# Layer 0's feed-forward of x by seven products, with the context's tokens as a stage of their own

## The chip, the cores and the metric

One Trainium2 chip, one core of it. The metric is device time of one launch, in microseconds (us); lower is better. The kernel before takes 2818.6 us, the median of three runs (2816.46 to 2821.4). The core has a matrix engine (TensorE, here PE), a vector engine (VectorE, DVE), an activation engine (ScalarE, ACT), GpSimd (POOL) and a queue engine (SyncE, SP) that issues the transfers in order. Sums are gathered in PSUM banks; a bank here holds 128 x 512 float32.

## The reference, cut to what matters

Two layers over 1024 tokens x and 256 context tokens h of width 1024, all in float32. Layer 0 mixes x and h and gives both new values; layer 1 gives only x. Each layer has six modulation vectors for x and for h, products of a condition with the columns of a 1024 x 6144 matrix.

```python
for layer in range(DEPTH):            # DEPTH = 2
    last = layer == DEPTH - 1
    mx = split(cond @ ada_w[layer] + ada_b[layer], 6)      # for x; mh the same of cond_ctx
    xn = modulate(rms(x, norm_mix[layer]), mx[0], mx[1])
    hn = modulate(rms(h, norm_mix[layer]), mh[0], mh[1])
    yx, yh = mixer(xn, hn, ..., not last)
    x = x + mx[2] * yx
    x = x + mx[5] * swiglu(modulate(rms(x, norm_ffn[layer]), mx[3], mx[4]), ffn_in[layer], ffn_out[layer])
    if not last:
        h = h + mh[2] * yh
        h = h + mh[5] * swiglu(modulate(rms(h, norm_ffn[layer]), mh[3], mh[4]), ffn_in[layer], ffn_out[layer])
return rms(x, norm_final)

def swiglu(x, w_in, w_out):           # w_in 1024 x 5632, w_out 2816 x 1024
    a, b = split(x @ w_in, 2)
    return (silu(a) * b) @ w_out
```

## The kernel before

Activations are stored with features on the 128 partitions: x[c] is [128, 8, n], eight blocks of 128 features by n tokens, for three chunks c: the halves 0 and 1 of x (n = 512) and the context 2 (n = 256). A float32 product is made of three matmuls (`mm3`, L111 to L114): each operand is cut into a high part and a remainder, and high x high, remainder x high and high x remainder are added in one PSUM bank. A weight block of 128 x 1024 (512 KB) is loaded by SP (`load_w`), its high part made by ACT (`split`, L103) and the remainder by POOL (L109) or DVE (L107). `mm_blk` runs the eight feature blocks of one weight block over one chunk, 24 matmuls.

Layer 0's end, in the order of the code:

- `MixerOut.sweep` makes the mixer's output, one block of 128 output features at a time; the first sweep is over chunk 0, the second over chunks 1 and 2 together, so the eight weight blocks are loaded twice. Each block is added to x and its squares are collected for the norm (`Rms`). `norm` puts the normalising and cutting of a chunk (line L239 and following, tiles `a`) on a list of deferred work, which later blocks pop.
- `ffn` runs over 22 blocks of 128 hidden features, and in each over the three chunks. `f_in` makes two times 24 matmuls of the first product, then SiLU (ACT, L843), the gate (DVE, L844) and the cut into `hh` and `hl`. `f_out` makes 24 matmuls of the second product, eight outputs of three, each added at once to x by DVE (L861). The three weight blocks of a hidden block are shared by the three chunks.
- `ada_bg(1)`, called after each step of `ffn`, works off one modulation block of layer 1: SP loads two halves of 256 KB, DVE makes a dot product of each with the condition (L149).
- `final0` interleaves the last hidden block with the first four weight blocks (10 to 13) of layer 1's mixer input.

Layer 1's feed-forward, for x only, already goes by seven products: each of the two matrix products is split in 2 x 2 (halves of the inner dimension by halves of x), and seven products of sums of the parts take the place of eight. The parts of the normalised x are called B11, B21, T2, T3, T1, T4, B22. `front_1` and `front_2` make the two products that can begin before the second half of x is there, the `Block` methods the other five, and a hidden block of x takes 7 x 12 = 84 matmuls in place of 96. The out stage (`fout`, 42 steps of seven products by six groups of hidden blocks, written (product, group)) makes 924 matmuls where the plain form has 1056. In it each step's operands are loaded from two buffers in DRAM, `sd` (sums of weights) and `hd` (sums of hidden values), and cut by ACT (L1675) and DVE (L1676).

A scheduler sets the order of the instructions on every engine except between `manual_schedule` marks, where the written order holds; each queue then runs in order.

Of the kernel before, what the change touches and what calls it, by code (L numbers as in the profile page):

```python
# [19 lines left out]
P = 128  # L20
D = 1024
# [18 lines left out]
def dit(ctx, tc, A, out):  # L40
# [790 lines left out]
    def ffn(l, xn, cs, after, done, final, bg=None):  # L831
        steps = [(j, c) for j in range(NJ - 1) for c in cs]
        wts, hid = {}, {}

        def f_in(j, c):
            n = CH[c][1]
            if j not in wts:
                wts[j] = [load_w(A["w_fi"][l, j, i]) for i in range(2)] + [load_w(A["w_fo"][l, j])]
            first = j == 0 and c == cs[0]
            pa = mm_blk(wts[j][0], c, xn, first)  # L840
            pb = mm_blk(wts[j][1], c, xn, False)
            s = t2k()
            ac.activation(s[:, :n], pa, AF.Silu)  # L843
            ve.tensor_tensor(s[:, :n], s[:, :n], pb, op=ALU.mult)  # L844
            hh = T(pw, [P, 512], "hh", F32R, 3)
            hl = T(pw, [P, 512], "hl", F32R, 3)
            split(hh[:, :n], hl[:, :n], s[:, :n])
            hid[j, c] = hh, hl
            run_deferred()

        def f_out(j, c, part=None):
            n = CH[c][1]
            s = slice(0, n) if part is None else part
            hh, hl = hid[j, c]
            wh, wl = wts[j][2]
            for m in range(KB):
                ps = T(pp, [P, 512], "ps")
                ms = slice(m * P, m * P + P)
                mm3(ps[:, s], wh[:, ms], wl[:, ms], hh[:, s], hl[:, s], True, True)
                xm = x[c][:, m, s]  # L860
                ve.scalar_tensor_tensor(xm, ps[:, s], mod(l, which(c), GATE_F, m), xm, op0=ALU.mult, op1=ALU.add)  # L861
                if j == NJ - 1:
                    after(c, m, s)
            if j == NJ - 1:
                done(c, s)

        for i, st in enumerate(steps):
            f_in(*st)
            if i:
                f_out(*steps[i - 1])  # L870
            if bg is not None:
                bg()
        final(f_in, f_out, lambda: f_out(*steps[-1]))

# [4 lines left out]
    for c in (1, 2):  # L879
        acts[c] = load_act(c, ocd)  # L880
        load_x_res(c)
    mo.sweep([0], acts)
# [6 lines left out]
    for typ in (GATE_M, SCALE_F, SHIFT_F, GATE_F):  # L889
        ada_queue(1, typ, ["x"])  # L890
    rm1 = {}
    xd = [T(dram, [P, 8, 512], f"xd{c}") for c in range(2)]

    def after0(c, m, s):
        if m == 0:
            rm1[c] = Rms(CH[c][1], 1024, KB, 3 if c == 1 else 0)
        rm1[c].add(x[c][:, m])
        if m == KB - 1 and c < 2:
            sy.dma_start(xd[c], x[c])

    xn1 = {}

    def done0(c, s):
        norm_apply(xn1, rm1[c], x[c], c, 1, SCALE_M, SHIFT_M)
# [46 lines left out]
    def final0(f_in, f_out, prev):  # L951
        wis = [10, 11, 12, 13]
        wt = {}

        def blk(i, c):
            wi = wis[i]
            if i not in wt:
                wt[i] = load_w(A["w_cd"][wi])
            epis[wi](0, c, mm_blk(wt[i], c, xn1, False))

        f_in(NJ - 1, 2)
        prev()
        f_in(NJ - 1, 0)
        f_out(NJ - 1, 2)
        f_out(NJ - 1, 0)
        run_deferred()
        f_in(NJ - 1, 1)
        blk(0, 2)
        f_out(NJ - 1, 1)
        blk(1, 2)  # L970
        blk(2, 2)
        blk(0, 0)
        run_deferred()
        for i, c in ((1, 0), (2, 0), (3, 2), (3, 0), (0, 1), (1, 1), (2, 1), (3, 1)):
# [202 lines left out]
    class Halves:  # L1177


        def __init__(self, *tags):  # L1180
            self.h = [T(pX, [P, 4, 512], t, F32, 2 if t == "w1" else 1) for t in tags]

        def __getitem__(self, ix):
            p, m, *s = ix
            a = m.start if isinstance(m, slice) else m
            h = a // 4
            m = slice(m.start - 4 * h, m.stop - 4 * h) if isinstance(m, slice) else m - 4 * h
            return self.h[h][(p, m, *s)]

    x = [Halves("w1", "rx"), Halves("w1", "wo")]  # L1190
# [217 lines left out]
    xr = [T(dram, [P, 8, 512], f"xr{c}") for c in range(2)]  # L1408

    def cut(hi, lo, src, leng, bias=None):  # L1410

        b = 0.0 if bias is None else bias
        ac.activation(hi, src, AF.Identity, bias=b)  # L1413
        if bias is None:
            (ve if leng == "dve" else po).tensor_tensor(lo, src, f32(hi), op=ALU.subtract)  # L1415
        else:
            ve.scalar_tensor_tensor(lo, src, b, f32(hi), op0=ALU.add, op1=ALU.subtract)

    class Seven:

        def __init__(self, l, xs_, alloc):
            self.l, self.x, self.t, self.alloc = l, xs_, {}, alloc
            sh = mods[l, SHIFT_F]
            self.sh = [sh[:, k, 0:1] for k in range(KB)]
            d = T(cst, [P, 4, 1], f"dsh{l}")
            ve.tensor_tensor(d, sh[:, 4:8, 0:1], sh[:, 0:4, 0:1], op=ALU.subtract)
            self.d = [d[:, k] for k in range(4)]

        def scaled(self, c, r, k):
            y = self.x[c][:, k]
            ve.scalar_tensor_tensor(y, y, mod(self.l, "x", SCALE_F, k), r.r, op0=ALU.mult, op1=ALU.mult)

        def new(self, name):
            self.t[name] = self.alloc(name)

        def parts(self, name, at, raws, bias=None):

            self.new(name)  # L1440
            hi, lo = self.t[name]
            todo = None
            for k in range(4):
                if at:
                    at(name, k)
                s = raws(k)
                b = bias(k) if bias else 0.0
                ac.activation(hi[:, k], s, AF.Identity, bias=b)
                if todo:
                    todo()  # L1450

                def todo(k=k, s=s, b=b):
                    if bias:
                        ve.scalar_tensor_tensor(lo[:, k], s, b, f32(hi[:, k]), op0=ALU.add, op1=ALU.subtract)
                    else:
                        ve.tensor_tensor(lo[:, k], s, f32(hi[:, k]), op=ALU.subtract)

            todo()

        def first(self, r):  # L1460
            for k in range(KB):
                self.scaled(0, r, k)
            self.parts("B11", None, lambda k: self.x[0][:, k], lambda k: self.sh[k])
            self.parts("B21", None, lambda k: self.x[0][:, k + 4], lambda k: self.sh[k + 4])

        def second(self, r, tmp, at):
            x0, x1, sh = self.x[0], self.x[1], self.sh
            t2 = {}

            def sub(o, a, b, c_):  # L1470
                ve.scalar_tensor_tensor(o, a, b, c_, op0=ALU.add, op1=ALU.subtract)
                return o

            def r2(k):
                self.scaled(1, r, k)
                self.scaled(1, r, k + 4)
                ve.tensor_tensor(x0[:, k], x1[:, k], x0[:, k], op=ALU.subtract)
                t2[k] = tmp()
# [14 lines left out]
    for m in range(KB):  # L1493
        spill(0, m)
# [502 lines left out]
```

## Time and profile before

| | |
|---|---|
| time of the runs shown, median | 2818.6 us |
| the profiled execution's own time | 2822.97 us |
| its span | 2821.2 us |
| PE busy | 2663.8 us, 94% |
| DVE busy | 1802.2 us, 64% |
| ACT busy | 1033.1 us, 37% |
| POOL busy | 668.3 us, 24% |
| DMA | 300.45 MB, 106 GB/s in the mean |

Times are counted from the span's start. The mixer's output of layer 0 lies at about 590 to 680 us, layer 0's feed-forward at 683 to 1620, layer 1's mixer at 1620 to 2150 and its feed-forward from there to the end. PE, DVE, ACT and POOL are busy with data; SP only issues. The granted clock tells how much of a stretch PE ran at the higher of its two levels (1.2 and 2.4 GHz). What an engine waited for is put down to the last thing that came.

### The profile page before, as it was taken

How to read it: one execution, taken by the hardware profiler on the slowest of the kernel's cores; microseconds unless marked ns; L12 is line 12 of the kernel's file. 1: busy time of each engine (PE TensorE's matmuls, PEld its weight loads, DVE VectorE, ACT ScalarE, POOL GpSimd, SP SyncE). 2: the span in 40 equal slices, each digit the busy share in tenths (PEclk: the TensorE clock that was granted, in tenths of full speed). 3: DMA queues.
4: the chain of work that ended last, by engine and by line, in shares of the span. 5: the costliest groups of instructions: out<-in, count | busy, mean ns of one | idle time of the engine just before them, and what ended most of it. 6: DMA issues, size and time to landing. Idle time of an engine off the chain costs nothing.

```text
span 2821.2 us, 35301 instructions
## 1 busy us (share of the span) xinstructions
PE 2663.8 (94%) x13524; PEld 2237.7 (79%) x13524; DVE 1802.2 (64%) x3170; ACT 1033.1 (37%) x1677; POOL 668.3 (24%) x438
## 2 busy tenths in 40 slices
PE   6988899999999999999999899898899899999998
PEld 4877788787888888888888788787667688888886
DVE  7769776556665555555444635887767766665555
ACT  5425455543111111111111532676654333332443
POOL 2132122352121211112111415643320121102110
PEclk8999999999999999999999899999999999999999
DMA  6343110352122122222111122113351444446653
GB/s 239 104 130 122 38 31 27 113 174 75 60 82 75 54 90 68 75 68 76 37 38 45 62 103 88 57 61 124 111 176 64 142 160 172 157 171 242 223 190 136
DMA packets 127929, 300.45 MB, mean 106 GB/s; under 512 B 12176, under 2 KB 28304, under 8 KB 126480
## 3 DMA queue, kind: packets, MB, share of 16 engines
q1 hardware_dynamic: 126512, 296.62, 31.5%
q8 instruction: 106, 1.74, 0.3%
q10 hardware_dynamic: 1248, 1.57, 0.2%
q14 instruction: 63, 0.52, 0.1%
HBM read 240.22 MB, written 57.93 MB: 106 GB/s over the span
## 4 chain that ended last, share of the span: by engine, by line
PE 68%; DVE 16%; DMA 6%; ACT 5%; issue 3%; POOL 2%; SPq 0%; DVEq 0%; ACTq 0%; POOLq 0%
PE ps L112 21%; PE ps L113 21%; PE ps L114 21%; DVE junk L149 3%; DMA adaw<-in_ada_dram 2%; PE ps L702 1%; DVE sm L1100 1%; DVE t2k L234 1%; DVE st L682 1%; DVE spt L107 1%; ACT P L685 1%; PE ps L192 1%; POOL wl L109 1%; DMA t2k<-oc 1%; ACT wh L103 1%
## 5 line engine op out<-in xcount | busy, mean ns | idle before, releaser
L112 PE MATMUL ps<-a,wh 128*128 128x512 f32 (+1 forms) x1784 | 656.5, 368 | 19.3 <-ACT a L239 6.9
L113 PE MATMUL ps<-a,wl 128*128 128x512 f32 (+1 forms) x1784 | 649.7, 364 | 10.2 <-DVE wl L107 9.1
L114 PE MATMUL ps<-a,wh 128*128 128x512 f32 (+1 forms) x1784 | 648.2, 364 | 2.4 <-DVE a L240 1.8
L109 POOL TENSOR_TENSOR wl<-raw,wh 128x1024 fp32r<-128x1024 f32 x109 | 269.0, 2471 | 863.2 <-ACT wh L103 856.7
L112 PEld LDWEIGHTS ps<-a,wh 128*128 128x128 f32 x1784 | 342.2, 192 | 78.1 <-ACT a L239 8.8
L113 PEld LDWEIGHTS ps<-a,wl 128*128 128x128 f32 x1784 | 342.2, 192 | 67.1 <-DVE wl L107 12.3
L114 PEld LDWEIGHTS ps<-a,wh 128*128 128x128 f32 x1784 | 342.0, 192 | 55.0 <-DVE a L240 3.1
L861 DVE SCALAR_TENSOR_TENSOR x<-ps,md,x 128x512 f32<-128x512 f32 (+1 forms) x528 | 312.2, 652 | 4.4 <-PE ps L114 4.4
L149 DVE CUSTOM_DVE_ANT_0 junk<-adaw,cond_x 128x512 bf16<-128x512 f32 x160 | 137.9, 862 | 171.6 <-DMA adaw<-in_ada_dram 169.7
L844 DVE TENSOR_TENSOR t2k<-t2k,ps 128x512 f32<-128x512 f32 (+1 forms) x66 | 39.3, 596 | 246.0 <-PE ps L114 246.0
L112 PE MATMUL ps<-hh,wh 128*128 128x512 f32 (+1 forms) x528 | 188.7, 357 | 3.0 <-ACT hh L103 2.1
L114 PE MATMUL ps<-hl,wh 128*128 128x512 f32 (+1 forms) x528 | 187.6, 356 | 1.1 <-DVE hl L107 1.1
L113 PE MATMUL ps<-hh,wl 128*128 128x512 f32 (+1 forms) x528 | 188.3, 357 | 0.0
L843 ACT ACTIVATE t2k<-ps 128x512 f32<-128x512 f32 (+1 forms) x66 | 34.8, 527 | 380.8 <-PE ps L114 380.8
L103 ACT ACTIVATE wh<-raw 128x1024 fp32r<-128x1024 f32 x127 | 133.9, 1056 | 108.2 <-PE ps L114 37.9
L1537 POOL TENSOR_TENSOR wo<-wo 128x512 f32<-128x512 f32 x44 | 76.9, 1749 | 403.4 <-DMA wo<-in_w_fo_dram 400.8
L112 PE MATMUL ps<-a,w 128*128 128x512 f32 x400 | 158.0, 395 | 7.6 <-ACT w L1413 6.3
L113 PE MATMUL ps<-a,w 128*128 128x512 f32 x400 | 157.8, 395 | 1.5 <-DVE w L1415 1.5
L114 PE MATMUL ps<-a,w 128*128 128x512 f32 x400 | 157.6, 394 | 0.0
L103 ACT ACTIVATE hh<-t2k 128x512 fp32r<-128x512 f32 (+1 forms) x66 | 36.8, 557 | 285.4 <-DVE t2k L844 285.4
L112 PEld LDWEIGHTS ps<-hh,wh 128*128 128x128 f32 x528 | 100.6, 190 | 18.5 <-ACT hh L103 2.6
L114 PEld LDWEIGHTS ps<-hl,wh 128*128 128x128 f32 x528 | 100.5, 190 | 15.6 <-DVE hl L107 1.5
(379 smaller groups left out, 5612.5 us busy)
## 6 DMA issues: line engine op xcount, KB each, us to landing
adaw<-in_ada_dram SPq DMA_DIRECT2D x160, 256.0 KB, 2.7
raw<-in_w_fi_dram SPq DMA_DIRECT2D x72, 512.0 KB, 3.6
hd<-t2k SPq DMA_DIRECT2D x66, 256.0 KB, 6.0
raw<-hd SPq DMA_DIRECT2D x28, 512.0 KB, 4.9
raw<-in_w_cd_dram SPq DMA_DIRECT2D x26, 512.0 KB, 3.5
raw<-in_w_fo_dram SPq DMA_DIRECT2D x22, 512.0 KB, 3.6
wo<-in_w_fo_dram SPq DMA_DIRECT2D x22, 512.0 KB, 5.4
sd<-wo SPq DMA_DIRECT2D x11, 1024.0 KB, 7.1
```

Of the source, the lines that this page charges most:

```text
L103: ac.activation(hi, src, AF.Identity)
L107: ve.tensor_tensor(lo, src, f32(hi), op=ALU.subtract)
L109: po.tensor_tensor(lo, src, f32(hi), op=ALU.subtract)
L112: te.matmul(ps, wh, xh, start=first, stop=False, skip_group_check=more)
L113: te.matmul(ps, wl, xh, start=False, stop=False, skip_group_check=more)
L114: te.matmul(ps, wh, xl, start=False, stop=last, skip_group_check=more)
L149: ve.tensor_tensor_reduce(jk[:, :512], w, cond[which][:, h * 512 : h * 512 + 512], op0=ALU.mult, op1=ALU.add, scale=1.0, scalar=0.0, accum ...
L192: te.matmul(self.ps, ones, sq[:, :n], start=self.count == 1, stop=self.count == self.total)
L843: ac.activation(s[:, :n], pa, AF.Silu)
L844: ve.tensor_tensor(s[:, :n], s[:, :n], pb, op=ALU.mult)
L861: ve.scalar_tensor_tensor(xm, ps[:, s], mod(l, which(c), GATE_F, m), xm, op0=ALU.mult, op1=ALU.add)
L1537: e.tensor_tensor(self.rows(o, o + 1), self.rows(a, a + 1), self.rows(b, b + 1), op=op)
```

## The change

Layer 0's feed-forward of x goes by seven products as layer 1's does. The classes of layer 1 (`Halves`, `Seven`, `Back`, `Block`) are moved up, take the layer as an argument, and serve both layers. Around them:

- The mixer's output takes three sweeps: chunk 0, then the context, then chunk 1; the eight weight blocks are loaded a third time. Both halves of x are stored to DRAM (`spill`, to xr00 and xr01).
- The context's tokens have a stage of their own before x's: 22 steps of two input products and one output product of 256 columns (`ctx_in`, `ctx_out`), with weight blocks loaded and cut for them alone (`ctx_load`, remainders on DVE). Its eight outputs are gathered in four PSUM banks over all 22 steps. Beside it, parts of x are prepared (`t1_raw`, `t3_raw`, T2, `pre_w`), and the modulation blocks still queued are worked off.
- Then x's front products, its parts T3, T1, T4, B22, the main stage over 22 hidden blocks (`main`), and the out stage (`out`). In the out stage the context's values are read back from DRAM and normalised, and 32 modulation blocks of layer 1 are worked off (`ada_one`: one load of 512 KB, one dot product of 1024, two buffers), two per step from step (2,4) on.
- Weight blocks 10 and 11 of layer 1's mixer input follow, then 12, 13 and the rest.

Layer 0's feed-forward weights are thus read from DRAM twice. The core of the diff:

```diff
-    for c in (1, 2):
+    for c in (2, 1):
         acts[c] = load_act(c, ocd)
         load_x_res(c)
+    sv = Seven(0, x, pX, None, 3)
...
     mo.sweep([0], acts)
     mo.w.update((m, load_w(mo.wsrc(m), "dve")) for m in range(2))
-    mo.norm(0)
-    mo.sweep([1, 2], acts)
-    mo.norm(1)
+    for m in range(KB):
+        sv.spill(0, m)
...
+    deferred.append(first0)
+    mo.sweep([2], acts)
+    mo.w.update((m, load_w(mo.wsrc(m), "dve")) for m in range(2))
+    sy.dma_start(xc0, x[2])
     mo.norm(2)
+    mo.rm[1] = Rms(512, 1024, KB, 2)
+    for m in range(KB):
+        mo.block(m, 1, acts)
+        sv.spill(1, m)
+        ada_bg(1)
...
+    def ctx_load(j, what):
+        if what == "fi":
+            t = act_tile(0, [P, 2, 2, 1024])
+            hi, lo = t[:, 0], t[:, 1]
+        else:
+            t = sv.t8([P, 2, 1024])
+            hi, lo = t[:, 0:1], t[:, 1:2]
+        for i in range(2 if what == "fi" else 1):
+            raw = T(pC, [P, 1024], "cr", F32, 3)
+            mark[0] = sy.dma_start(raw, A["w_fi"][0, j, i] if what == "fi" else A["w_fo"][0, j]).ins
+            cut(hi[:, i], lo[:, i], raw)
+        cw[what, j] = hi, lo
...
+    for j in range(NJ):
+        ctx_in(j)
+        ctx_load(j, "fo")
+        if j + 2 < NJ:
+            ctx_load(j + 2, "fi")
+        if j:
+            ctx_out(j - 1)
...
+        if 2 <= j < 6:
+            sv.t1_raw(mo.rm[1], j - 2)
+            sv.t3_raw(j - 2)
+        if j > 5:
+            ada_bg(1)
...
+    sv.second(None, None, ("T2",), True)
+    ctx_out(NJ - 1)
...
+    for j in range(3):
+        sv.front_1(j)
+        sv.front_2(j)
...
+    sv.second(None, None, ("T3",), True)
...
+    d = T(pW, [P, 8, CTX], "w34", F32, 3)
+    for m in range(KB):
+        ac.activation(d[:, m], couts[m // 2][:, m % 2 * CTX : m % 2 * CTX + CTX], AF.Identity, scale=mod(0, "c", GATE_F, m))
+    sy.dma_start(dc0, d)
...
+    sv.main(bl)
...
+    def ada_one(typ, b):
+        w = T(pX, [P, 2, 1024], "w1", F32, 2)[:, 0]
+        sy.dma_start(w.rearrange("p (h n) -> p h n", h=2), A["ada"][1, typ * KB + b].rearrange("h p n -> p h n"))
+        m_ = mod_tile(1, typ)
+        ve.tensor_tensor_reduce(adc[:, 1], w, adc[:, 0], op0=ALU.mult, op1=ALU.add, scale=1.0, scalar=0.0,
+                                accum_out=m_[:, b, 0:1])
...
+        if (i, b) > (2, 3):
+            for _ in range(2):
+                if ada_tail:
+                    ada_one(*ada_tail.pop(0))
+        if i == 6 and b in (1, 3):
+            pre_cd(10 + b // 2)
...
+    sv.out(x, [slice(0, 512)], added0, ended0, bg0)
...
-    ffn(0, xn, [0, 1, 2], after0, done0, final0, lambda: ada_bg(1))
-    ada_bg(1000)
```

What this moves on the queues, at the places where the stages meet. SP, in the changed kernel, at the end of the sweep over chunk 1 and the start of the context's stage (L827 stores a block of x, L1295 loads a weight block of the context's stage into a raw tile `cr`; a name after "waits" is what the issue waits for):

```order
L827 DMA xr01_1009_5232<-wo_967_5117 128x512 [waits DVE_49]
L1295 DMA cr_1189_6234<-in_w_fi_dram 128x1024 [waits Pool_49]
L827 DMA xr01_1009_5232<-wo_967_5117 128x512 [waits DVE_49]
L1295 DMA cr_1190_6238<-in_w_fi_dram 128x1024 [waits DMAHW4_49,PE_49]
L1295 DMA cr_1192_6243<-in_w_fi_dram 128x1024 [waits Pool_49]
```

The second half of the first weight block is issued behind the store of x's last block.

DVE in the out stage, from layer 1 in the kernel before (L1676 cuts a step's operands, L1866 adds an output to x):

```order
L1676 TENSOR_TENSOR a_3678_21742<-raw_21739,a_3678_21742 128x2048
L1676 TENSOR_TENSOR a_3680_21772<-raw_21769,a_3680_21772 128x2048
L1866 SCALAR_TENSOR_TENSOR a_3647_21437<-ps_21617,md_2148_11755,a_3647_21437 128x512
L1866 SCALAR_TENSOR_TENSOR a_3647_21437<-ps_21618,md_2148_11755,a_3647_21437 128x512
L1866 SCALAR_TENSOR_TENSOR a_3647_21437<-ps_21619,md_2148_11755,a_3647_21437 128x512
L1866 SCALAR_TENSOR_TENSOR a_3647_21437<-ps_21620,md_2148_11755,a_3647_21437 128x512
L1676 TENSOR_TENSOR tx_21806<-rx_21802,tx_21805 128x2048
```

and from layer 0 in the changed kernel (L773 is the cut, L1462 the dot product of a modulation block and its read-out):

```order
L773 TENSOR_TENSOR tx_12280<-raw_12276,tx_12279 128x2048
L1462 ISA wo_11393,md_1864_12247<-w_1865_12249,wo_11393 128x1024
L1462 ISA md_1864_12247 128x1
L773 TENSOR_TENSOR a_1872_12316<-rx_12313,a_1872_12316 128x2048
L1462 ISA wo_11393,md_1864_12247<-w_1869_12283,wo_11393 128x1024
L1462 ISA md_1864_12247 128x1
```

Between the cuts stand one or two dot products, where layer 1 has none.

SP at the same place of the changed kernel (L1053 and L1059 load a step's operands, L1460 a modulation block):

```order
L1053 DMA raw_1860_12238<-sd02_1018_5241 128x1024 [waits DMAHW4_49,DVE_49]
L1460 DMA w1_1855_12181<-in_ada_dram 128x2x512 [waits DMAHW1_49,DVE_49]
L1460 DMA w1_1858_12214<-in_ada_dram 128x2x512 [waits DMAHW2_49,DVE_49]
L1059 DMA raw_1860_12238<-hd02_1012_5235 128x1024 [waits DMAHW7_49]
L1053 DMA raw_1866_12276<-sd03_1019_5242 128x1024 [waits DMAHW0_49,Activation_49]
L1460 DMA w1_1859_12217<-in_ada_dram 128x2x512 [waits DMAHW5_49,DVE_49]
L1460 DMA w1_1863_12245<-in_ada_dram 128x2x512 [waits DMAHW6_49,DVE_49]
L1059 DMA raw_1866_12276<-hd03_1013_5236 128x1024 [waits DMAHW3_49]
```

The second load of each step's operands is issued behind two modulation loads that wait for DVE.

## Rows read from the trace of the kernel before

**Rows 1.** the profile's page, busy time of the engines, then the chain by engine

```profile
PE 2663.8 (94%) x13524; PEld 2237.7 (79%) x13524; DVE 1802.2 (64%) x3170; ACT 1033.1 (37%) x1677; POOL 668.3 (24%) x438
...
PE 68%; DVE 16%; DMA 6%; ACT 5%; issue 3%; POOL 2%; SPq 0%; DVEq 0%; ACTq 0%; POOLq 0%
```

**Rows 2.** busy time by stretch: stretch, length, engines' busy us (instructions), clock, DMA share, GB/s

```profile
core 0: us, PE busy (x) PEld busy (x) DVE busy (x) ACT busy (x) POOL busy (x), PEclk, DMA share, GB/s
550.00:690.00 140.00, 131.96 (x655) 111.39 (x655) 72.50 (x110) 59.37 (x86) 65.45 (x37) 0.98 0.47 154
690.00:823.00 133.00, 128.02 (x657) 108.13 (x656) 91.92 (x170) 29.83 (x46) 22.81 (x9) 1.00 0.19 58
823.00:1560.00 737.00, 737.00 (x3882) 637.42 (x3881) 402.65 (x696) 111.81 (x162) 132.41 (x54) 1.00 0.20 63
1560.00:1640.00 80.00, 69.54 (x308) 56.40 (x307) 50.80 (x77) 45.38 (x72) 27.13 (x21) 0.89 0.21 81
...
2150.00:2235.00 85.00, 72.19 (x289) 55.47 (x288) 68.24 (x94) 37.25 (x55) 6.52 (x5) 0.94 0.34 118
2235.00:2580.00 345.00, 345.00 (x1503) 282.30 (x1502) 222.56 (x270) 115.01 (x160) 66.89 (x39) 1.00 0.44 158
2580.00:2790.00 210.00, 209.29 (x915) 171.49 (x914) 121.55 (x85) 84.03 (x65) 22.93 (x12) 1.00 0.66 226
2600.00:2650.00 50.00, 50.00 (x222) 41.38 (x221) 23.36 (x15) 18.13 (x11) 0.00 (x0) 1.00 0.77 274
```

**Rows 3.** timeline of PE in layer 0's feed-forward: start, duration, operation; then its SiLUs

```profile
915.13 0.39 PE L114 MATMUL ps<-hl,wh 128*128 128x512 f32 x1
...
915.81 0.39 PE L114 MATMUL ps<-hl,wh 128*128 128x512 f32 x1
916.03 0.28 PE L112 MATMUL ps<-a,wh 128*128 128x256 f32 x1
...
916.27 0.28 PE L114 MATMUL ps<-a,wh 128*128 128x256 f32 x1
...
L843 ACT ACTIVATE t2k<-ps x4: 383/598/598, 905.4 to 946.7; 128x512 f32<-128x512 f32 x3, 128x256 f32<-128x256 f32 x1
```

**Rows 4.** layer 1: one line's instructions in 2340:2364, another's in 2725:2742

```profile
L1731 DVE TENSOR_TENSOR t2k<-ps,t2k x2: 690/690/691, 2343.8 to 2363.1; 128x512 f32<-128x512 f32 x2
...
L1675 ACT ACTIVATE tx<-raw x2: 1917/1918/1918, 2728.2 to 2733.6; 128x2048 fp32r<-128x2048 f32 x2
```

**Rows 5.** what PE waited for in 550:690, 1560:1640, 2150:2235: us, times, longest

```profile
PE ps L112 <- ACT a L239: 5.1, 1, 5.1
PE ps L113 <- DVE wl L107: 1.6, 1, 1.6
PE ps L112 <- ACT wh L103: 1.3, 1, 1.3
...
PE ps L112 <- ACT t2k L935: 5.6, 1, 5.6
...
PE ps L112 <- ACT w L1413: 6.3, 1, 6.3
```

**Rows 6.** cuts and dot products, by line: count, min/median/max ns, first and last start

```profile
L103 ACT ACTIVATE wh<-raw x127: 1040/1061/1078, 205.0 to 2129.0; 128x1024 fp32r<-128x1024 f32 x127
...
L109 POOL TENSOR_TENSOR wl<-raw,wh x109: 2347/2400/3801, 206.1 to 1974.4; 128x1024 fp32r<-128x1024 f32 x109
...
L107 DVE TENSOR_TENSOR wl<-raw,wh x18: 1212/1224/2299, 595.6 to 2130.1; 128x1024 fp32r<-128x1024 f32 x18
...
L1676 DVE TENSOR_TENSOR a<-raw,a x15: 2283/2292/2907, 2579.9 to 2786.1; 128x2048 fp32r<-128x2048 f32 x15
...
L340 DVE CUSTOM_DVE_ANT_0 junk<-a,cond_x x12: 1211/1220/2173, 12.5 to 52.4; 128x1024 bf16<-128x1024 f32 x12
```

**Rows 7.** DMA issues: count, KB each, median us from issue to landing

```profile
raw<-in_w_fi_dram SPq DMA_DIRECT2D x72, 512.0 KB, 3.6
...
wo<-in_w_fo_dram SPq DMA_DIRECT2D x22, 512.0 KB, 5.4
```

More of the change, by code (lines that the diff above doesn't have):

```diff
@@ L829, in norm_apply @@
         deferred.append(later)
[L831 to L873, printed above, removed]
     mo = MixerOut(0, lambda m: A["w_abo"][m])
@@ L891, in dit, with first0 @@
[L891 to L904 removed]
+    for m in range(KB):
+        sv.spill(0, m)
+    def first0():
+        mo.rm[0].finish()
+        sv.first(mo.rm[0])
@@ new lines, in dit, with at0 @@
+    sy.dma_start(dc0, d)
+    sv.load_fi(2)
+    sv.front_s(0)
+    bk.part(3)
+    sv.front_3(0)
+    bl = Block(sv, 0, bk)
+    sv.front_s(1)
+    bk.part(4)
+    sv.second(None, None, ("T1",), True)
+    bl.m6()
+    bl.m7()
+    sv.front_3(1)
+    sv.front_s(2)
+    bl.u1()
+    def at0(name, k):
+        if (name, k) == ("T4", 0):
+            bl.m5()
+        if (name, k) == ("T4", 2):
+            sv.front_3(2)
+            bl.z7()
+        if (name, k) == ("B22", 0):
+            bl.m4()
+        if (name, k) == ("B22", 1):
+            bl.c22()
@@ L906, in dit @@
+    sv.second(None, at0, ("T4", "B22"), True)
+    sv.load_fi(3)
+    sv.main(bl)
+    sM.close()
+    sW.close()
+    sB0 = es()
+    pxB = pool(sB0, "pxB")
+    x = [T(pxB, [P, 8, 512], f"xb{c}") for c in range(2)]
+    for c in range(2):
+        sy.dma_start(x[c], sv.xr[c])
+    xd = [T(dram, [P, 8, 512], f"xd{c}") for c in range(2)]
+    rm1, xn1 = {}, {}
+    rm1[0] = Rms(512, 1024, KB, 2)
+    rm1[1] = Rms(512, 1024, KB, 3)
     zd = {nm: T(dram, [P, k, 1280], f"z{nm}") for nm, k in (("rk", 2), ("rq", 2), ("rg", 4), ("rv", 4))}
@@ L1175, in dit @@
     pX = pool(sX, "pX", side="right")
[L1177 to L1190, printed above, removed]
+    x = list(halves(pX))
     t2_pool(sF, "t2j", t2k=5)
@@ L1407, in dit @@
     mo.load(1)
[L1408 to L1478, printed above, removed]
-                sub(t2[k], x1[:, k + 4], sh[k + 4], x0[:, k])
-                return t2[k]
-            self.parts("T2", at, r2)
-            self.parts("T3", at, lambda k: sub(x1[:, k], x1[:, k + 4], self.d[k], x1[:, k]))
-            self.parts("T1", at, lambda k: x0[:, k])
-            self.parts("T4", at, lambda k: sub(x0[:, k + 4], x0[:, k + 4], sh[k + 4], t2[k]))
-            self.parts("B22", at, lambda k: x1[:, k + 4], lambda k: sh[k + 4])
@@ L1882, in dit, with added1, ended1 @@
-    fout(1)
+    def added1(i, c, m, s):
+        if i in (1, 5):
+            rm1[0].add(x[0][:, m])
+        if i == 4:
+            for q_ in range(2):
+                rm1[1, q_].add(x[1][:, m, cuts[q_]])
+        if i == 6:
+            rm1[1, s.start // 256].add(x[1][:, m, s])
+    def ended1(i, s):
+        if i == 3:
+            for q_ in range(2):
+                rm1[1, q_] = Rms(256, 1024, KB, 3)
+        if i == 5:
+            done1(0, slice(0, 512), rm1[0])
+        if i == 6:
+            done1(1, s, rm1[1, s.start // 256])
@@ L1883, in dit @@
+    sv.out(x, cuts, added1, ended1)
     sA.close()
```

833 lines of the change are left out of this document (490 added, 343 removed).

## The prediction

> **What bounds the kernel now.** I read the busy line and the chain of waits first, then the busy time by stretch, the pace of TensorE (PE) inside the stretches, and last what PE waited for in the stretches that are not full. PE is busy 94% of the span, and 68% of the chain that ended last is PE [rows 1]. By stretches [rows 2]: in layer 0's feed-forward (823 to 1560 us) PE is busy for all 737 us at a granted clock of 1.00, with DMA at 0.20 and VectorE (DVE) at 403 of 737; layer 1's main stage (2235 to 2580) and its out stage (2580 to 2790) are full too. So here a matmul taken away is time taken away. The rest is at the seams. I count a stretch's loss as its length less PE's busy time, plus (1 - granted clock) x length, since at the lower of the two clock levels (1.2 against 2.4 GHz) half of the time is lost, and the share of time there is twice (1 - clock). That gives 8.0 + 2.8 = 10.8 us for 550:690, 5.0 for 690:823, 10.5 + 8.8 = 19.3 for 1560:1640, and 12.8 + 5.1 = 17.9 for 2150:2235, layer 1's change from its mixer to seven products.
>
> **Pace.** A 512-column matmul starts every 0.227 us (915.13 to 915.81 is three), a 256-column one every 0.12 (916.03 to 916.27 is two) [rows 3]. One hidden block of layer 0 has 144 of the first and 72 of the second: 32.7 + 8.6 = 41.3 us, which is the distance of the first and last SiLU of one chunk in the row of four [rows 3]. In layer 1, 84 matmuls of a hidden block take 2363.1 - 2343.8 = 19.3 us, 0.230 each, and an out step of 24 takes 2733.6 - 2728.2 = 5.4 [rows 4].
>
> **What goes.** Each hidden block of x drops from 96 to 84 matmuls of the first product: 22 x (96 x 0.227 - 19.3) = 22 x 2.44 = 53.7 us, taking layer 1's measured pace for the new code, which is the same code. The second product drops from 1056 to 924 matmuls: 132 x 0.227 = 29.9. Together -83.6 us. The 528 additions on DVE that went with every out product go too, but PE did not wait for them (DVE is at 55% there), so they count as nothing; neither do the 64 modulation blocks' halves that DVE did in that stretch.
>
> **Mixer out in three sweeps and the seam to the feed-forward.** Before, PE stood 5.1 us for the normalised x and 1.6 + 1.3 us for the first weights of the sweep [rows 5]. The norm now lies under the next sweep, so the 5.1 goes, and so does the slow start of 690:823; the 2.9 us stay. New: the context's sweep alone gives PE only 24 x 0.12 = 2.9 us per weight block, where a cut takes 1.06 on ScalarE (ACT) and 2.4 on GpSimd (POOL) [rows 6]. That fits under 2.9 with four buffers, barely: between 0 and 8 us (eight blocks of 1 us, as for a load that lands 3.6 us after its issue [rows 7] with one block of lead); I take 2. What is late next is the first weight of the context stage: in SP's order its second half stands behind the last spill of x, and its tile is free only when the sweep ends. Landing, cut and remainder are 3.6 + 1.06 + 1.22 = 5.9 us [rows 6, 7]; between 3 and 8, I take 5. So 15.8 becomes 9.9: -5.9 us.
>
> **The context's stage.** 22 steps of 72 matmuls of 256 columns, 8.6 us each, the same PE work as before, now without x's matmuls beside it. Per step three weight blocks: ACT 3 x 1.06 = 3.2, DVE 3 x 1.22 = 3.7 plus about one for the hidden values and about one for x's own preparation in some steps, and 1.57 MB in 8.6 us = 182 GB/s. The nearest row is layer 1's out stage: 226 GB/s with PE full [rows 2]. Three raw buffers and 5.9 us from issue to ready give 3 blocks per 5.9 us. Between 0 and 10 us in all; I take 1.
>
> **The change to seven products.** Layer 1's own lost 17.9 us, 6.3 of it for one cut of weights [rows 2, 5]. Here T2, the front weights and the first raw blocks are made beforehand under the context's stage; but T3, T1, T4 and B22 are made while PE waits for each, and the context's eight outputs are drained by ACT in between. Between 5 and 18; I take 12.
>
> **The out stage with 32 modulation blocks.** In the row order 27 of them lie between steps (3,0) and (5,3): 14 full steps and two halves, 14 x 5.4 + 2 x 2.7 = 81 us of PE. DVE: layer 1's out stage uses 121.6 of 210 us, so 47 of 81, and 27 dot products x 1.22 = 33 [rows 2, 6]: 80 of 81. Bytes: 226 GB/s x 81 us = 18.3 MB and 27 x 0.524 = 14.2, 32.5 MB. Where the share was 0.77 the DMAs moved 274 GB/s [rows 2], so 356 at a full share: 91 us. The two buffers: one pair takes a landing plus a dot product, 3.6 or 5.4 + 1.22 = 4.8 to 6.6 us [rows 6, 7], 13.5 pairs in 65 to 89. Three resources thus lie at the length of the stage itself, and some 11 us (two steps) are buffered ahead. A wait is added on SP: the load of the hidden sums for the step after next is queued behind two modulation loads that wait for DVE, and DVE's remainder for that step, then PE, stand behind it. Lower end 0; upper end with pair and remainder in series, (5.4 + 1.22 + 2.29) x 13.5 = 120, +39. I take 12, nearest to the DMA rows.
> The Trainium skill, "DMA: Bandwidth & Descriptors", section "Where 436 GB/s comes from", lets about 358 GB/s per core bind for HBM to SBUF, and its section on measured bandwidth has 425 for one core alone with a 16 MB transfer. The first agrees with the 356 worked out above; by 425 the 32.5 MB would need 76 us, the DMAs would not bind, and the forecast would be 2732; no row here shows such a rate.
>
> **The tail.** 19.3 us were lost at 1560:1640, 5.6 of them in one wait on ACT [rows 5]. Now the last four sums wait for squares, the first four blocks of the next projection (16.6 us on ready columns) cover the last norm, and one more weight load stands behind a store. Left: between 4 and 15; I take 9: -10.3 us.
>
> **Sum.** -83.6 - 5.9 + 1 + 12 + 12 - 10.3 = -74.8 us. The profiled execution took 2823.0 (span 2821.2 and 1.8 around it), 0.16% over the median of 2818.6; 2823.0 - 74.8 = 2748.2, in the median's terms 2744. With all terms at their lower ends: -83.6 - 9.9 + 0 + 5 + 0 - 15.3 = -104, 2715; at their upper ends: -83.6 + 3.1 + 10 + 18 + 39 - 4.3 = -18, 2801.
>
> **Rivals.**
> (a) The out stage is paced by the modulation blocks: pair and remainder in series, +39 in place of 12, 2771. For it: DVE at 80 of 81 us, two buffers, and one SP queue in which loads wait behind waiting loads. Against: the scheduler spread the pairs, and steps are cut two ahead.
> (b) Slower than before: the context's stage is paced by its weights. One mechanism: with PE giving only 8.6 us per block, three loads and their cuts go through the ring one after the other, 3 x (3.6 + 1.06) = 14 us per block [rows 6, 7]; 22 x 5.4 = +118, 2862. It decides from 8.6 + 75/22 = 12 us per block. For it: weights that x's matmuls used to cover are now read for 256 columns alone; tiles for the first product are two, freed only when a block's product ends. Against: three raw buffers, and 5.9 us from issue to ready.
> (c) The seams cost what they did: starts, transition and tail at their upper ends with the out stage at 12, -83.6 + 3.1 + 10 + 18 + 12 - 4.3 = -45, 2774. For it: each new seam brings its own starting waits and low clock (0.89 and 0.94 at the old ones [rows 2]). Against: the pieces are prepared under the stage before.
>
> **Chances.** Forecast 0.67, (a) 0.15, (b) 0.07, (c) 0.11. Its own range is 2720 to 2766; 8 in 10 with (a) and most of (c): 2720 to 2785. About 0.2% is what a measurement of this kernel can tell from no change. Faster by over that: all but (b) and a sliver between (c) and (b), 0.90; within it 0.03; slower 0.07, case (b).
>
> **What would show it.** The main stage of layer 0 with 19.3 us between its C21 additions; PE full from the second context step on, 8.6 us a step; gaps of PE in steps (3,0) to (5,3) that end with a DMA or a DVE remainder, 12 us in sum; 5 us before the first context product; about 12 us lost between the last context product and the first steady block. Wrong if context steps are over 9.2 us, if those 16 out steps take over 110 us, or if the main block's distance is over 19.8.

## The result, and the profile after

The changed kernel takes 2789.2 us in the median (2782.7 to 2794.1, four runs) against 2820.0 of the kernel before, a ratio of 0.989 with the interval 0.9865 to 0.9915. It is faster by 31 us, where 75 were forecast (2744, range 2720 to 2785). Its profiled execution took 2782.7 (span 2780.9) and is the quickest of the four; a second profile of the same kernel (below) has a span of 2790.8.

The page after: span, busy time, granted clock by slice, and the chain by engine.

```profile
span 2780.9 us, 34949 instructions
...
PE 2593.3 (93%) x13136; PEld 2167.0 (78%) x13136; DVE 1863.8 (67%) x2986; ACT 1209.7 (44%) x1859; POOL 597.8 (21%) x416
...
PEclk8999999998999999999999999999999999999999
...
PE 57%; DVE 20%; DMA 10%; issue 6%; ACT 5%; POOL 1%; SPq 1%; DVEq 0%; ACTq 0%; POOLq 0%
```

PE lost 70 us of busy time (84 went with the matmuls, but more of what is left ran at the lower clock: granted 0.974 in the mean, before 0.980), and the span only 40; DVE's share of the chain rose from 16 to 20% and DMA's from 6 to 10% [rows 1]. The stretches after, with the columns of [rows 2]:

```profile
677.00:692.00 15.00, 0.18 (x1) 0.18 (x1) 9.09 (x23) 4.23 (x5) 1.65 (x2) 0.65 0.52 178
692.00:702.00 10.00, 9.32 (x55) 9.03 (x56) 5.93 (x5) 5.77 (x6) 0.00 (x0) 0.67 0.76 256
...
820.00:893.00 73.00, 73.00 (x603) 72.37 (x601) 42.52 (x53) 36.52 (x55) 0.00 (x0) 1.00 0.53 168
...
905.00:928.00 23.00, 17.14 (x71) 13.31 (x70) 19.11 (x28) 11.65 (x18) 1.45 (x1) 0.91 0.38 137
928.00:1310.00 382.00, 380.37 (x1644) 309.31 (x1642) 241.57 (x297) 125.09 (x175) 67.56 (x40) 1.00 0.45 160
...
1327.00:1350.00 23.00, 23.00 (x103) 18.99 (x102) 9.91 (x9) 10.83 (x14) 7.54 (x7) 1.00 0.95 377
...
1475.00:1500.00 25.00, 21.07 (x88) 16.49 (x86) 20.27 (x25) 6.87 (x7) 7.46 (x3) 0.95 0.86 298
1500.00:1525.00 25.00, 20.50 (x72) 15.72 (x73) 18.60 (x15) 14.83 (x12) 4.13 (x2) 0.85 0.91 316
...
1557.00:1593.00 36.00, 29.32 (x147) 23.93 (x145) 12.23 (x18) 13.21 (x20) 4.80 (x2) 0.95 0.30 103
```

The main stage (928 to 1310) is full, and its block distance is the one that layer 1 showed [rows 4], by DVE's C21 additions (first and last start of two):

```profile
L1154 DVE TENSOR_TENSOR t2k<-ps,t2k x2: 692/692/692, 1001.0 to 1020.4; 128x512 f32<-128x512 f32 x2
```

1020.4 - 1001.0 = 19.4 us. So the 84 us of matmuls were saved as forecast; the difference is at the places that are not full. I compare each stretch with the pure time of its matmuls (0.227 and 0.12 us each; the main stage at 19.3 per block), by the starts of PE's first instruction of each stage (within the out stage by counting its matmuls), in the first and second profile of the changed kernel:

| stretch | pure work | first profile | second | lost | forecast loss |
|---|---|---|---|---|---|
| mixer output to first context product | 121.3 | 143.9 | 146.1 | 22.6, 24.8 | 9.9 |
| context's stage | 190.1 | 197.8 | 196.3 | 7.7, 6.2 | 1 |
| fronts, parts and main stage | 424.6 | 437.2 | 437.6 | 12.6, 13.0 | 12 |
| out stage, steps (3,0) to (5,3) | 81.7 | 89.8 | 93.8 | 8.1, 12.1 | 12 |
| rest of the out stage, to its last sum | 128.0 | 140.9 | 144.3 | 12.9, 16.3 | in the next line |
| first 17 blocks of the next projection | 79.7 | 91.8 | 91.9 | 12.1, 12.2 | 9 |

(121.3 is the kernel before's own 132.1 us less the 10.8 it lost there.) 76 or 85 us are lost where 44 were forecast; before it was 35. The forecast put the modulation blocks into the steps (3,0) to (5,3), and what follows them, with the waits for sums of squares, into the tail. Some 7 us of the rest of the out stage are no waiting but PE's own matmuls for these sums (L213, fifteen of about 0.46 us in the trace). What PE waited for up to the end of the context's stage, the four largest:

```profile
PE ps L113 <- ACT a L771: 15.2, 1, 15.2
PE ps L113 <- ACT wh L104: 4.7, 1, 4.7
PE ps L114 <- POOL wl L110: 3.7, 2, 2.1
PE ps L115 <- DVE ch L773: 2.5, 2, 1.5
```

and from the out stage to the next projection, the three largest (us in total, times, longest), where [rows 5] had one wait of 5.6 at the tail:

```profile
PE ps L113 <- ACT wh L104: 6.7, 1, 6.7
PE ps L213 <- POOL g L204: 4.5, 2, 3.6
PE ps L113 <- ACT a L771: 3.7, 1, 3.7
```

**The first seam.** DVE at the end of the third sweep: start, duration, line, operation.

```profile
659.12 2.77 DVE L150 CUSTOM_DVE_ANT_0 junk<-adaw,cond_c 128x512 bf16<-128x512 f32 x1
...
681.85 1.41 DVE L150 CUSTOM_DVE_ANT_0 junk<-adaw,cond_x 128x512 bf16<-128x512 f32 x1 [0.66 <-DMA adaw<-in_ada_dram]
...
683.30 0.69 DVE L150 CUSTOM_DVE_ANT_0 junk<-adaw,cond_c 128x512 bf16<-128x512 f32 x1
...
685.38 1.41 DVE L1222 SCALAR_TENSOR_TENSOR wo<-ps,md,wo 128x512 f32<-128x512 f32 x2
691.80 1.23 DVE L773 TENSOR_TENSOR a<-cr,a 128x1024 fp32r<-128x1024 f32 x1 [5.01 <-ACT a L771]
```

L1222 is the residual addition of two output blocks of the mixer. PE ended the last of them by 676.7; the additions start at 685.4, behind dot products of modulation blocks (L150), one of which waited 0.66 us for its load. Most of these take 0.69 us; the one at 659.1 and another at 663.6 took 2.77, each beside a remainder on POOL:

```profile
658.48 2.85 POOL L110 TENSOR_TENSOR wl<-raw,wh 128x1024 fp32r<-128x1024 f32 x1
```

These two are some 4 us of DVE's time ahead of the last additions; whether POOL is the cause was not tried. SP at the end of the sweep:

```profile
686.15 0.33 SPq L827 DMA_DIRECT2D xr<-wo  x1
686.53 0.42 SPq L1295 DMA_DIRECT2D cr<-in_w_fi_dram  x1
687.00 0.46 SPq L827 DMA_DIRECT2D xr<-wo  x1
```

The stores of x (L827) wait for these additions, and the first weights of the context's stage (L1295) stand between and behind them: cut on ACT at 690.7, product at 691.8. From the issue at 686.5 to the product it is 5.3 us; the rest of the wait is the late issue. After this standstill PE ran at a granted clock of 0.67 for the next 10 us, two thirds of them at the lower of its levels (1.2 GHz): an estimated 3.3 us more.

**The out stage.** DVE and then SP near the step that PE waited for:

```profile
1492.08 1.23 DVE L1462 CUSTOM_DVE_ANT_0 wo<-w,wo 128x1024 f32<-128x1024 f32 x1 [1.70 <-DMA w<-in_ada_dram]
...
1494.44 1.23 DVE L1462 CUSTOM_DVE_ANT_0 wo<-w,wo 128x1024 f32<-128x1024 f32 x1 [1.13 <-DMA w<-in_ada_dram]
...
1497.38 1.23 DVE L1462 CUSTOM_DVE_ANT_0 wo<-w,wo 128x1024 f32<-128x1024 f32 x1 [1.71 <-DMA w<-in_ada_dram]
...
1498.53 2.29 DVE L773 TENSOR_TENSOR a<-raw,a 128x2048 fp32r<-128x2048 f32 x1
```

```profile
1488.10 2.69 SPq L1460 DMA_DIRECT2D w<-in_ada_dram  x2
1490.84 0.46 SPq L1059 DMA_DIRECT2D raw<-hd  x1
1493.34 2.73 SPq L1460 DMA_DIRECT2D w<-in_ada_dram  x2
```

Each dot product (L1462) waits for its load, 1.1 to 1.7 us, and DVE's remainder of a step's operands at 1498.5 (L773) comes behind them. SP issues the next pair (1493.3) only when a dot product has given back its buffer (1493.2; the two buffers, used in turn, are called the ring below), and a step's loads stand behind or between such pairs: the one of its hidden sums was issued at 1490.8 (L1059). ACT waited for it to make the high part, and PE's two waits at this step were for both cuts:

```profile
1495.73 1.91 ACT L771 ACTIVATE a<-raw 128x2048 fp32r<-128x2048 f32 x1 [10.86 <-DMA raw<-hd]
...
PE ps L114 <- DVE a L773: 1.1, 1, 1.1
```

PE's wait of 3.7 us ended with ACT's high part (1497.6), that is with a load held up on SP's queue; 1.1 us more went to DVE's remainder behind the dot products. In the second profile the two are 6.1 and 2.3 us (the latter in two waits).

### The profile page after: what moved, and what is told of

Read it like the earlier page. It is cut to its first block, busy times and chain, and to the rows that moved or that the text cites. A ratio compares the mean times of both kernels' runs of the same rounds, so it can differ in the third digit from the quotient of the medians.

```text
span 2780.9 us, 34949 instructions
## 1 busy us (share of the span) xinstructions
PE 2593.3 (93%) x13136; PEld 2167.0 (78%) x13136; DVE 1863.8 (67%) x2986; ACT 1209.7 (44%) x1859; POOL 597.8 (21%) x416
## 4 chain that ended last, share of the span: by engine, by line
PE 57%; DVE 20%; DMA 10%; issue 6%; ACT 5%; POOL 1%; SPq 1%; DVEq 0%; ACTq 0%; POOLq 0%
PE ps L115 17%; PE ps L114 17%; PE ps L113 17%; DMA adaw<-in_ada_dram 3%; DVE junk L150 3%; DMA rx<-hd 1%; DMA w<-in_ada_dram 1%; DVE a L773 1%; PE ps L703 1%; DVE sm L1647 1%; DMA raw<-in_w_abo_dram 1%; DVE st L683 1%; DVE spt L108 1%; DMA raw<-in_w_cdo_dram 1%; ACT P L686 1%
## 5 line engine op out<-in xcount | busy, mean ns | idle before, releaser
L113 PE MATMUL ps<-a,w 128*128 128x512 f32 (+1 forms) x864 | 340.3, 394 | 14.2 <-ACT w L771 11.3
L114 PE MATMUL ps<-a,w 128*128 128x512 f32 (+1 forms) x864 | 339.5, 393 | 1.7 <-DVE w L773 1.7
L115 PE MATMUL ps<-a,w 128*128 128x512 f32 (+1 forms) x864 | 338.8, 392 | 0.0
L113 PE MATMUL ps<-a,wh 128*128 128x512 f32 (+1 forms) x680 | 265.1, 390 | 15.3 <-ACT wh L104 14.7
L114 PE MATMUL ps<-a,wl 128*128 128x512 f32 (+1 forms) x680 | 261.1, 384 | 16.3 <-DVE wl L108 10.2
L115 PE MATMUL ps<-a,wh 128*128 128x512 f32 (+1 forms) x680 | 259.1, 381 | 0.2 <-DVE a L108 0.2
L113 PEld LDWEIGHTS ps<-a,w 128*128 128x128 f32 x864 | 163.5, 189 | 51.9 <-ACT w L771 12.1
L114 PEld LDWEIGHTS ps<-a,w 128*128 128x128 f32 x864 | 163.6, 189 | 38.4 <-DVE w L773 2.8
L115 PEld LDWEIGHTS ps<-a,w 128*128 128x128 f32 x864 | 163.7, 189 | 36.2 <-DVE a L779 0.3
L773 DVE TENSOR_TENSOR w<-raw,w 128x1024 fp32r<-128x1024 f32 (+1 forms) x111 | 137.7, 1250 | 73.8 <-ACT w L771 73.8
L114 PEld LDWEIGHTS ps<-a,wl 128*128 128x128 f32 x680 | 133.5, 196 | 46.4 <-DVE wl L108 13.6
L113 PEld LDWEIGHTS ps<-a,wh 128*128 128x128 f32 x680 | 134.4, 198 | 42.6 <-ACT wh L104 16.2
L115 PEld LDWEIGHTS ps<-a,wh 128*128 128x128 f32 x680 | 133.9, 197 | 22.9 <-DVE a L108 0.6
L110 POOL TENSOR_TENSOR wl<-raw,wh 128x1024 fp32r<-128x1024 f32 x47 | 114.6, 2440 | 146.4 <-ACT wh L104 146.3
L115 PE MATMUL ps<-tx,w 128*128 128x512 f32 x352 | 140.5, 399 | 0.0
L113 PE MATMUL ps<-tx,w 128*128 128x512 f32 x352 | 138.6, 394 | 1.7 <-ACT t2k L1142 1.7
L114 PE MATMUL ps<-tx,w 128*128 128x512 f32 x352 | 138.9, 395 | 0.0
L114 PE MATMUL ps<-a 128*128 128x512 f32 (+1 forms) x324 | 128.9, 398 | 1.1 <-DVE a L773 1.1
L113 PE MATMUL ps<-a 128*128 128x512 f32 (+1 forms) x324 | 125.8, 393 | 3.7 <-ACT a L771 3.7
```

The source lines that it names most:

```text
L110: po.tensor_tensor(lo, src, f32(hi), op=ALU.subtract)
L113: te.matmul(ps, wh, xh, start=first, stop=False, skip_group_check=more)
L114: te.matmul(ps, wl, xh, start=False, stop=False, skip_group_check=more)
L115: te.matmul(ps, wh, xl, start=False, stop=last, skip_group_check=more)
L773: ve.tensor_tensor(lo, src, f32(hi), op=ALU.subtract)
```

## The experiments

All times but e11's (one run) are medians of four runs beside the kernel before on the same chip, whose medians there were 2820 to 2822; the changed kernel's is 2789. Out stage times are from its first to its last sum with the last twelve products of the main stage (+3 us), 233.7 and 241.1 us in the two profiles of the changed kernel.

**e1, no modulation blocks in the third sweep.** They go to the context's stage, where what is left of the list is worked off at the last step in place of step 10.

```diff
         sv.spill(1, m)
-        ada_bg(1)
...
+        if j == NJ - 1:
+            ada_bg(1000)
         if j == 10:
-            ada_bg(1000)
             sv.load_fi(0)
```

> The modulation blocks that stood in the mixer output's third sweep are worked off in the context's stage from its step 6 on. Theory (the dot products stand ahead of the residual additions in DVE's order, so the sweep's last additions, the stores of x and then the first weights come late): PE's wait before the first context product falls from 15.2 us to about 5, and the stretch from the start of the mixer output to that product from 143.9 us to about 133; time 9 to 12 us below the changed kernel's, about 2779. Rival (the wait is the landing and cutting of the first weights, behind the stores on SP's queue): the wait stays over 10 us and the time within 3 us of the changed kernel's.

2789.1 us, no change in the time, though the mechanism showed: the stretch to the first context product is 133.2 us in place of 143.9. PE's waits up to the end of the context's stage, two of its rows:

```profile
PE ps L115 <- DVE ch L773: 5.5, 6, 1.4
...
PE ps L113 <- ACT a L771: 3.9, 1, 3.9
```

The wait for the first weights is 3.9 us, and the context's stage now waits 5.5 for hidden values (`ch`), cut by DVE behind the same dot products: the stage takes 202.0 in place of 197.8. The out stage took 240.7, like the second profile of the changed kernel. Against that profile the edit is worth 5 us by the spans (2785.8 for 2790.8), which four runs spread over 10 do not show.

**e2, no modulation blocks in the out stage** (`ada_tail = []`).

> Left out: the 32 modulation blocks of layer 1 that the out stage works off (their results are set to zero). Theory (they are what the out stage loses): the loss of layer 0's out stage against its matmuls' pace falls from 21 us to 6 to 10 (the sums of squares at its end stay), the waits at 1494 to 1501 go; 10 to 14 us below the changed kernel, about 2777. Rival (the loss comes from the step loads themselves and from the end of the stage): at most 4 us.

2777.1 us, 12 below. The out stage took 225.9. So the 32 blocks cost 8 to 15 us there, as work that PE has to wait for. The steps (3,0) to (5,3) took 82.0 us, PE's own pace; 4.4 us of waits for sums of squares stayed at the end of the stage.

**e3, the weights behind the out stage.**

```diff
-    wpools[:] = [(pwA, 2, 1), (pwB, 2, 1)]
+    wpools[:] = [(pwB, 2, 1), (pwA, 2, 1)]
     wnext[0] = 0
     wh_ = {wi: load_w(A["w_cd"][wi]) for wi in (12, 13, 0)}
```

> The first weight block behind the out stage's four is loaded into the pool whose memory is free earlier, the other one second. Theory (PE's 6.7 us wait there is the load behind the last store on SP, into memory that the products before still used): the wait goes to under 1 us, 6 to 8 us below the changed kernel, about 2782. Rival (the wait moves to the next weight block, which is now the late one): the time stays within 2 us.

2778.9 us, 10 below. All that PE waited for from 1560 to 1660:

```profile
PE ps L213 <- POOL g L204: 0.9, 1, 0.9
```

The wait of 6.7 us for the weights is gone and no other took its place; the first 17 blocks of the next projection take 80.8 us in place of 91.8.

**e4, the modulation loads issued by GpSimd.**

```diff
-        sy.dma_start(w.rearrange("p (h n) -> p h n", h=2), A["ada"][1, typ * KB + b].rearrange("h p n -> p h n"))
+        po.dma_start(w.rearrange("p (h n) -> p h n", h=2), A["ada"][1, typ * KB + b].rearrange("h p n -> p h n"))
```

> The loads of the 32 modulation blocks in the out stage are issued by GpSimd in place of SP; the same bytes, the same dot products. Theory (PE's waits at 1494 to 1501 come from step loads queued on SP behind modulation loads that wait for their buffer): these 5 us go, about 5 us below the changed kernel, 2784. Rival (the DMAs, 0.85 to 0.95 busy there, or DVE are the limit): the time stays within 2 us, with waits in other steps.

2804.5 us, 15 above: a miss of both. SP's loads no longer stood behind the modulations, and yet the out stage took 255.6 us. DVE there:

```profile
1424.41 2.72 DVE L1094 SCALAR_TENSOR_TENSOR xb<-ps,md,xb 128x512 f32<-128x512 f32 x4
1427.05 1.22 DVE L1462 CUSTOM_DVE_ANT_0 wo<-w,wo 128x1024 f32<-128x1024 f32 x1
...
1428.30 1.23 DVE L1462 CUSTOM_DVE_ANT_0 wo<-w,wo 128x1024 f32<-128x1024 f32 x1
...
1431.99 2.29 DVE L773 TENSOR_TENSOR a<-raw,a 128x2048 fp32r<-128x2048 f32 x1 [2.45 <-ACT a L771]
...
1436.40 1.22 DVE L1462 CUSTOM_DVE_ANT_0 wo<-w,wo 128x1024 f32<-128x1024 f32 x1
```

Both dot products of a pair stand between a step's additions (L1094) and the next cut, the next follows 8 us later, and a full step of PE takes 5.4. In the stage PE waited 10.2 us for DVE's remainders of `tx`, and DVE 39.9 us for modulation blocks (15.7 and 21.2 in the two profiles of the changed kernel). But the edit changes more than SP's queue: the loads now stand in GpSimd's order among the additions of squares, for which PE waited 9.6 us (4.5 and 7.1 before the edit). So e4 does not tell what SP's order costs in the changed kernel; it shows that modulation blocks that come late hold the stage through DVE as well.

**e5, a ring of four.** The two buffers are twice as large as a block; both halves are used.

```diff
+    ring = [None]
+
     def ada_one(typ, b):
-        w = T(pX, [P, 2, 1024], "w1", F32, 2)[:, 0]
+        if b % 2 == 0:
+            ring[0] = T(pX, [P, 2, 1024], "w1", F32, 2)
+        w = ring[0][:, b % 2]
```

> In the out stage both halves of each of the two buffers hold a modulation block, so four can be under way in place of two; the same loads, bytes and dot products, on SP as before. Theory (a dot product at the head of DVE's order waits for a block that could only be asked for when a buffer came free, and the cuts of the next step stand behind it): the out stage from its first to its last product falls from 234 to 242 us to about 230, and the time is 8 to 10 us below the changed kernel, about 2780. Rival (the DMAs at 0.85 to 0.9 busy are the limit): within 3 us of the changed kernel.

2769.2 us, 20 below, twice what was expected. The out stage took 221.3. Three stretches of it, first the changed kernel's second profile, then e5:

```profile
1400.00:1450.00 50.00, 50.00 (x221) 41.17 (x220) 41.88 (x56) 18.12 (x18) 0.00 (x0) 1.00 0.82 282
1450.00:1500.00 50.00, 46.23 (x202) 37.46 (x200) 38.76 (x47) 14.76 (x11) 7.27 (x3) 1.00 0.84 299
1500.00:1550.00 50.00, 39.16 (x143) 29.67 (x144) 34.24 (x37) 27.57 (x27) 6.30 (x2) 0.83 0.60 216
```

```profile
1400.00:1450.00 50.00, 50.00 (x221) 41.17 (x220) 46.33 (x66) 21.03 (x18) 0.00 (x0) 1.00 0.95 340
1450.00:1500.00 50.00, 50.00 (x221) 41.23 (x220) 44.81 (x47) 18.97 (x15) 6.67 (x3) 1.00 0.95 345
1500.00:1550.00 50.00, 48.56 (x211) 37.57 (x210) 31.94 (x36) 25.72 (x30) 5.12 (x3) 1.00 0.39 146
```

With the same work PE is full to 1500, and the DMAs move 340 and 345 GB/s where they moved 282 and 299. They had room: the limit was how early a block could be asked for. Of the 20 us, 12 lie in the steps (3,0) to (5,3), 82.0 us for 93.8, as without the blocks (e2); 8 lie behind them. Nearly all of these steps, in the changed kernel (first profile) and in e5:

```profile
1417.00:1498.60 81.60, 77.91 (x340) 63.94 (x340) 64.59 (x80) 25.30 (x17) 7.46 (x3) 0.99 0.89 310
...
1417.00:1498.60 81.60, 81.60 (x360) 67.25 (x359) 73.12 (x86) 30.99 (x21) 6.67 (x3) 1.00 0.96 350
```

The end of the stage gains too: its waits for sums fall from 7.1 us to 1.4, and the clock stays at 1.00 from 1500 to 1550 where it was 0.83.

**e6, half of the blocks in the sweep** (`if m < 4: ada_bg(1)`, the rest in the context's stage).

> Only the first four blocks of the third sweep are followed by a modulation block; the other four are made in the context's stage, one per step from step 6 on. Theory (the dot products ahead of the last additions delay the stage, and those in the context's stage cost where DVE has no room): the stretch to the first context product is about 134 us as with none in the sweep, the context's stage takes about 2 us more than the 197.8 of the changed kernel in place of 4.2, and the time is 6 to 9 us below the changed kernel, about 2782. Rival (whatever leaves the sweep is paid back in the context's stage): within 3 us of the changed kernel.

2777.4 us, 12 below, more than expected (its runs spread from 2774.6 to 2785.7, and the profiled one is the slowest). To the first context product 134.9 us, the context's stage 199.5.

**e7, e3, e5 and e6 together.**

> The other pool for the first weight block behind the out stage, the ring of four modulation blocks and the halved sweep together. Theory: the three act at different places, so the gains add: -10 - 9 - 7 = -26, about 2763. Rival (what is gained at one seam is waited for at the next): about 2772 or more.

2752.9 us (2749.9 to 2754.7), ratio to the kernel before 0.9755 (0.974 to 0.9771): 36 below the changed kernel, more than the 26 expected and less than the 10 + 20 + 12 = 42 of the three alone. The first seam takes 132.8, the out stage 221.6, and it is the best of all versions.

```profile
span 2752.9 us, 34933 instructions
...
PE 2588.9 (94%) x13136; PEld 2165.5 (79%) x13136; DVE 1864.5 (68%) x2986; ACT 1211.2 (44%) x1859; POOL 597.8 (22%) x416
```

**e8, the changed kernel again.**

> The changed kernel once more, beside the others. Theory (its out stage runs at the edge, where a landing more or less decides, and the profiled execution was one of the quicker ones): the out stage takes 234 to 243 us, the stretch to the first context product 143 to 145, the time about 2789. Rival (the profiled execution is typical): the out stage within 1 us of 233.7.

2789.0 us; out stage 241.1, first seam 146.1. e1, e3 and e6, which leave the out stage as it is, have 240.7, 241.7 and 242.2 there: the first profile was a quick one, by 7 us.

**e9 and e10, rings of three in the sweep and the context's stage.** `adaw` gets three buffers in place of two, on e7 (e9) and on e3 with e5, the sweep left whole (e10).

> The three edits together, and in the sweep and the context's stage a ring of three modulation halves in place of two. Theory (there too a dot product that waits for its load holds up DVE's queue; PE waited 4.2 us for hidden values in the context's stage): this wait falls to about 1 us, the stage from 200 to 197 us, 2 to 4 us below the three together, about 2750. Rival (DVE's work itself is too much there, whatever the loads): no change, 2753.

2757.4 us, 4 above e7 where 2 to 4 below were expected. PE's wait for hidden values grew from e7's 4.2 us:

```profile
PE ps L115 <- DVE ch L775: 7.5, 6, 1.5
```

> The other pool for the first weight block and the ring of four in the out stage; all eight modulation blocks stay in the third sweep, but with a ring of three halves. Theory (DVE's work and its place in the queue delay the sweep's last additions, the ring only in part): the stretch to the first context product falls from 144 us to about 140, PE's wait there from 13 to 9 us; about 2756. Rival (only the two-half ring delays them): about 134 us, as with four blocks in the sweep, about 2752.

2760.0 us; 142.7 us to the first context product (expected 140, by the rival 134; e5, with rings of two there, has the same 142.7), with a wait of

```profile
PE ps L113 <- ACT a L773: 11.6, 1, 11.6
```

So at the sweep and in the context's stage a ring of three does not help. In e10 DVE waits for no load from 655 us on (3.0 us in the changed kernel), and its last additions of the sweep still start only at 684.6 (685.4): there the dot products stand in the way by their place and their work (four of at least 0.7 us per block, for x and for the context). Of the three places only the out stage was held by its ring.

**e11, the kernel before again.**

> The kernel before once more, with a profile. From the first transposes behind layer 0 to the end it took 1125.9 us in its profile, and 1130 to 1135 in ten profiles of the changed kernel and its variants. Theory (the same code, another order of loads around it: a real 4 to 6 us): 1126 again. Rival (its first profile was a quick one): about 1130.

2820.7 us; 1128.9 us from the first transposes to the end, 3.0 more than in its first profile. So a part of the distance to the 1130 to 1135 of the changed kernel and its variants is spread between executions; a real part of up to a few us is not excluded, and its cause stays open.

## Why the prediction was wrong

- The matmuls taken away: right. 84 us, with the block distance at 19.4 against 19.3. (22 x (96 x 0.227 - 19.3) is 54.8, not 53.7: a slip of 1 us.)
- The transition to seven products: 12.6 us for 12, in part by luck. By the count that gave layer 1's 17.9, idle time plus low clock, 905:928 lost 5.9 + 2.1 = 8 us; the rest is mostly the main stage's (22 x 0.1 us of pace, 1.6 us idle).
- The first seam: this step failed. I priced the landing and cut of the first weights (5 us), and that is what they took once issued (5.3); PE waited 15.2, since they were issued late. The eight modulation blocks that the new sweep carries, four dot products each, were not counted at all, though they stand in the diff. They delay the last residual additions and with them the stores and the first load; e1 and e6 bring the wait to 3.9.
- The tail: this step failed too. I took 9 us, 15 at most; without the 7 us of PE's own sums it lost 18 and 22. Its terms were listed but too small: 6.7 us for the weight block behind a store, with the low clock that follows (e3 took 10 to 11 us of the tail), and 4.5 and 7.1 us for sums of squares, which I had named without a price. A part of this is handed on by the modulation blocks: e5 took 8 us behind the steps that hold them.
- The out stage: the size was right, 8 and 12 us for 12 in its sixteen steps, but by luck, for the reason was wrong. I took the 12 from the DMA rows, 91 us for 32.5 MB at 356 GB/s. The DMAs were not the limit: in e5 they move 350 GB/s through the same steps with PE full. The rate was about right there (350 at a share of 0.96), the bytes too high (350 GB/s x 81.6 us = 28.6 MB). What held the steps was the ring of two: e5, which changes only the number of blocks under way, runs them at PE's pace. The wait that I had added on SP, a step's load behind modulation loads that wait for DVE, is the larger part of what PE waited for, a remainder behind dot products the smaller; no run separates the two. Rival (a) names these same queues, but its size (+39) was too large, since pairs and cuts do overlap in part. On the rate of the DMAs, the Trainium skill, "DMA: Bandwidth & Descriptors", section on measured bandwidth, has 425 GB/s for a core alone; the 377 here (1327:1350, loads and stores) lies above the 358 of its section "Where 436 GB/s comes from", which was thus no limit in that stretch, and below the 425.
- The context's stage: 6 to 8 us for 1, by about 3.3 us of low clock behind the seam's wait and 1.2 to 2.5 of waits for hidden values behind dot products. Rival (b) is wrong: 820:893 is full, and the stage's 22 steps took 9.0 us each in the mean.
- In sum, 76 or 85 us were lost where 44 were forecast, 32 or 41 of the 44 us by which the time missed; some 6 us more lie behind the first transposes (e11), where I had expected nothing.
- Rival (c), 2774 with all seams at their upper ends, was nearer to the time than the forecast, and (a) too. With the first seam, the out stage's ring and the weights behind it mended, e7 reaches 2752.9, 9 us above the forecast.

## What to carry to other kernels

Background work on an engine that runs in order is not free because the engine has idle time: its place in the queue and the wait for its own load are passed on to whatever stands behind it. Count the instructions of such work at each seam, and ask how many of its loads can be under way: a load that can be asked for only when the one before last is used up sets the pace at landing time plus work, with bandwidth to spare. Work moved away from one seam can be paid for at the next: e1 saved 10.7 us at the first seam, gave back 4.2 in the context's stage, and its time did not fall; with half of the work moved (e6) it fell by 12.

## What the runs showed that was not expected

The changed kernel's out stage took 233.7 or 241.1 us with the same instructions, and its runs spread over 11 us; those of the kernel before spread over 6 beside them and over 10 to 12 beside the experiments. With the ring of four the spread is 3 us. Issuing 32 loads of 512 KB from GpSimd in place of SP cost 15 us, though GpSimd was busy only 21% of the span. Leaving out the modulation blocks (out stage 225.9) was slower there than keeping them with the ring of four (221.3); the steps that hold the blocks take 82.0 us in both, and PE waits 4.4 and 1.4 us for sums of squares at the end. Why the sums come later without the blocks was not tried.
